# State space branch of a hybrid decoder kernel kept with features on partitions, its norm factors spread by rows through DRAM

## The chip, the cores and the metric

One core of one Trainium2 chip runs the whole program. The metric is device time in microseconds (us), the median of repeated runs. Beside it stands one execution that the hardware profiler took. TensorE is called PE here, VectorE DVE, ScalarE ACT, GpSimd POOL; SP is the engine whose queue issues nearly all DMAs. A weight load is PE's fetch of a matmul's stationary operand.

## What is computed

A decoder trunk of two layers on 512 tokens of width 1024, in float32. Each layer projects the normed input once, feeds three branches (a state space branch, latent attention, a gated delta rule), merges them by sigmoid gates, and ends with a feed-forward block. The change lies in the state space branch:

```python
def ssd_mixer(z, xbc, dt_raw, conv_w, conv_b, dt_bias, a_log, d_skip, norm_g):
    xbc = jax.nn.silu(causal_dwconv(xbc, conv_w) + conv_b)
    xs, bm, cm = jnp.split(xbc, [SSD_INNER, SSD_INNER + G * N], axis=-1)
    dt = jax.nn.softplus(dt_raw + dt_bias).reshape(Bsz, S, G, E)
    a = -jnp.exp(a_log).reshape(G, E)
    y = ssd_chunked(xs * dt[..., None], dt * a, bm, cm)
    y = y + d_skip.reshape(G, E)[:, :, None] * xs
    y = y.reshape(Bsz, S, SSD_INNER) * jax.nn.silu(z)
    y = rmsnorm(y.reshape(Bsz, S, G, SSD_INNER // G), norm_g.reshape(G, SSD_INNER // G))
```

There are G = 2 groups of E = 8 heads of width 64, state width 128, and four chunks of 128 tokens. In a chunk the output is the sum of a part inside it (decay matrix times the product of `cm` and `bm`, times `xs * dt`) and a part from the state carried in (`cm` times state, times the decay since the chunk's start). The norm runs over the 512 features of a group, so it needs one factor for each token and group.

## The kernel before, in words

**Dense products.** Weights come in pieces of 512 KB by a DMA on SP's queue (`weights_raw`, L161, two buffers `wraw`). `split_half` makes of each half piece a high and a low part, `whi` by a copy on ACT (L154) and `wlo` by a subtraction on DVE (L155), four buffers each. `mm3` then issues three matmuls of 512 columns for each pair of 128x128 blocks (L182, L183, L184); these rows are called dense here. `dense_F` puts output features on partitions (the weights are the stationary operand), `dense_T` puts tokens there.

**The state space branch** is `ssd_group(g)`, called for g = 0 and 1 in each of two layers, four calls in all. It first projects `bm` and `cm` and, tile by tile, `xs`, with features on partitions; a convolution and SiLU follow (`conv_silu`, L682 to L686, `silu2`, L262 and L263). Four transposes on PE (L720) and a copy on ACT (L721) turn each tile of `xs` so that tokens are on partitions. The gate `z` is projected with `dense_T` (`silu_T`) and has tokens on partitions too.

Then four chunks t follow. `seg_exp` fetches cumulated log decays from DRAM tensor `d_c`, spread over all partitions (L448), and makes the decay matrices `eE` on ACT (L450, L451). PE multiplies `bm` by `cm` (L733); DVE masks the product and multiplies it into `eE` (L735, L737). DVE makes `xd`, that is `xs` times step size (L739), and the skip term (L744). For each of eight heads PE multiplies with `eE` as stationary and 64 columns of `xd` as moving operand (L742), so the result has tokens on partitions; DVE adds it (L745). From the second chunk on, one matmul of 512 columns brings in the state (L748), which DVE scales by a column of decays and adds (L750, L751). `xe` (L754) and one matmul of 512 columns (L756) make the next state (L759, L761, L762). At a chunk's end DVE multiplies into `z` (L764), and ACT squares it and sums along the row in the same instruction (L766), which gives the norm's sum for each token.

After the chunks `rsq` makes the factors with one DVE instruction and a power on POOL (L258, L259). DVE scales `z` (L770). Then the result is turned back, four transposes a tile on PE (L775), and `split_gain` makes high and low parts in `yh` and `yl` (L254, L255).

**What sets the order.** A scheduler at build time places the instructions of all branches in each engine's queue; every engine then works strictly through its own queue. The buffers of `yh` and `yl` hold latent attention's outputs until its output projection has read them, so the turned results of the branch wait for the end of that projection, and group 0's results stay in the `tok` buffers meanwhile. Around the chunks stand dense rows of attention's output projection (`out_proj`) and, after it, of the gated delta rule's keys.

Of the kernel before, what the change touches and what calls it, by code (L numbers as in the profile page):

```python
# [20 lines left out]
P = 128  # L21
S = 512
# [12 lines left out]
ROWS = ('ssd_dt_bias', 'gdn_dt_bias', 'ssd_a_log', 'gdn_a_log', 'ssd_d')  # L35
# [20 lines left out]
def hybrid_kernel(ctx, tc, a, out, depth=2, taps=None):  # L56
# [42 lines left out]
    ct = mk(cst, [P, NBLK * P + 104], F32, "ct")  # L99
# [195 lines left out]
    def load_params(ly, rows=True):  # L295
        pc = mk(sp, [P, 155], F32, "pc", 2)
        sync.dma_start(pc, a["pcols"][ly])
        prow = mk(sp, [P, 64], F32, "prow", 2)
        if rows:
            load_rows(prow, ly)  # L300
        return pc, prow
# [49 lines left out]
    for ly in range(depth):  # L351
# [5 lines left out]
        sconv_b, g_n1, g_ssd, g_q, g_kv, g_gdn, g_n2 = 0, 12, 20, 28, 32, 34, 35  # L357
# [32 lines left out]
        d_c = mk(dr, [T, 24 * P], F32, "d_c", 2)  # L390

        def step_sizes():
# [35 lines left out]
            sync.dma_start(d_c.rearrange("t (n l) -> (t n) l", l=P), rows)  # L428
            dec = mk(sp, [P, 3, T, 24], F32, "dec")
# [8 lines left out]
            dsk = mk(sp, [P, 16], F32, "dsk")  # L438
            dve.tensor_scalar(dsk, prow[:, 48:64], 0.25, None, ALU.mult)
# [257 lines left out]
        def ssd_group(g, yh, yl):  # L697
            h0 = 8 * g
            xs = mk(br, [P, T, 512], F32, "tok", 4)
            z = mk(br, [P, T, 512], F32, "tok", 4)  # L700
# [13 lines left out]
            for cp in range(2):  # L714
                for j, pj in enumerate(dense_F(weights(w_in, O_XBC + 512 * g + 256 * cp, 256, D), tiles(256), D, xh, xl)):
                    xf = mk(br, [P, S], F32, "ft4", 2)
                    conv(pj, 4 * g + 2 * cp + j, xf)
                    ps = sm_bank()
                    for t in range(T):
                        pe.transpose(ps[:, t * P : (t + 1) * P], xf[:, t * P : (t + 1) * P], ident)  # L720
                    act.copy(xs[:, :, (2 * cp + j) * P : (2 * cp + j + 1) * P], ps.rearrange("p (t n) -> p t n", t=T))  # L721
            silu_T(br, O_SZ + 512 * g, z)

            hv8 = lambda x: x.rearrange("p (h n) -> p h n", h=8)
            ss = mk(sp, [P, T], F32, "sss")
            st = None
            for t in range(T):
# [10 lines left out]
                xd = mk(br, [P, 512], F32, "wk0")  # L738
                dve.tensor_tensor(hv8(xd), hv8(xs[:, t, :]), bc_last(dtq[:, t, h0 : h0 + 8], 64), ALU.mult)  # L739
                py = sm_bank()  # L740
                for h in range(8):
                    pe.matmul(py[:, h * 64 : (h + 1) * 64], e2[h // 4][:, h % 4, :], xd[:, h * 64 : (h + 1) * 64], start=True, stop=True)  # L742
                y = mk(br, [P, 512], F32, "wk1")
                dve.tensor_tensor(hv8(y), hv8(xs[:, t, :]), bc_last(dsk[:, h0 : h0 + 8], 64), ALU.mult)  # L744
# [559 lines left out]
```

## Time and profile before

| | us |
|---|---|
| median of 3 runs (lowest, highest) | 2334.94 (2334.29, 2338.41) |
| the profiled execution | 2335.61 |
| its span, first to last instruction | 2333.8 |
| PE busy | 2290.0 |
| DVE busy | 1585.9 |
| ACT busy | 1177.4 |
| POOL busy | 59.1 |

So 1.8 us of the profiled execution lie outside its span. Matmuls are pipelined: a record's duration is longer than the time until the next one may start. What a matmul costs in a full queue is read from the distance between two starts. A float32 matmul leaves two records, a dense one (rounded float32) and a transpose one. The form `64*64 64x64` names the part of the array that a matmul uses (rows*columns), then the shape.

### The profile page before, as it was taken

The page shows a single profiled execution, that of the slowest core. Times are in us where ns is not written, and L with a number is a line of the kernel's source. Part 1 is how long each engine was busy: PE and PEld are TensorE (multiplying, and loading weights), DVE is VectorE, ACT ScalarE, POOL GpSimd, SP SyncE. Part 2 cuts the span into 40 slices and gives each one's busy share as a digit, 9 for nine tenths or more (in the row PEclk, how much of TensorE's full clock was granted, in tenths as well). Part 3 has the DMA queues.
Part 4 walks back from the last instruction along what each step waited for, and adds up shares of the span by engine and source line. Part 5 has one row for each costly group of instructions (what it writes and reads, how often), then busy time and mean ns, then how long its engine had stood idle before and what let it go on. Part 6 is the DMA issues. An engine that isn't in the chain of part 4 may idle for free.

```text
span 2333.8 us, 32026 instructions
## 1 busy us (share of the span) xinstructions
PE 2290.0 (98%) x11814; PEld 1884.8 (81%) x11814; DVE 1585.9 (68%) x3116; ACT 1177.4 (50%) x2455; POOL 59.1 (3%) x74
## 2 busy tenths in 40 slices
PE   8999999999999999999999999999999999999998
PEld 7878788878887888888887787888788878888886
DVE  7776666775665458767867765667656645677668
ACT  6666644333443345554656667443334434545545
POOL 0000000000000000000000000000000000000000
PEclk9999999999999999999999999999999999999999
DMA  4223533442222443233132235334422224333231
GB/s 136 83 73 91 171 100 109 122 132 79 80 78 69 148 144 109 74 116 118 51 97 72 74 99 163 105 103 140 115 83 85 68 80 155 127 117 100 91 109 46
DMA packets 208702, 239.85 MB, mean 103 GB/s; under 512 B 33888, under 2 KB 157472, under 8 KB 208544
## 3 DMA queue, kind: packets, MB, share of 16 engines
q1 hardware_dynamic: 205344, 233.07, 33.0%
q10 hardware_dynamic: 3200, 4.72, 0.8%
q8 instruction: 93, 1.52, 0.3%
q14 instruction: 65, 0.53, 0.1%
HBM read 221.41 MB, written 11.63 MB: 100 GB/s over the span
## 4 chain that ended last, share of the span: by engine, by line
PE 88%; DVE 6%; DMA 2%; ACT 2%; POOL 1%; issue 1%; ACTq 0%; SPq 0%; DVEq 0%; POOLq 0%
PE acc L182 23%; PE acc L183 22%; PE acc L184 22%; PE sm L182 2%; PE sm L184 2%; PE sm L183 2%; DVE wlo L155 1%; PE sm L742 1%; DMA eE<-d_c 1%; PE sm L645 1%; DVE tok L858 1%; DVE gQ L857 1%; PE sm L1015 1%; POOL gms L259 1%; PE yt L661 1%
## 5 line engine op out<-in xcount | busy, mean ns | idle before, releaser
L155 DVE TENSOR_TENSOR wlo<-wraw,whi 128x512 fp32r<-128x512 f32 (+1 forms) x552 | 376.5, 686 | 421.7 <-ACT whi L154 407.1
L154 ACT CAST whi<-wraw 128x512 fp32r<-128x512 f32 (+1 forms) x552 | 339.9, 618 | 593.4 <-PE acc L183 384.2
L184 PE MATMUL acc<-xh,wlo 128*128 128x512 f32 (+1 forms) x1248 | 486.3, 390 | 0.0
L182 PE MATMUL acc<-xh,whi 128*128 128x512 f32 (+1 forms) x1248 | 486.0, 390 | 0.0
L183 PE MATMUL acc<-xl,whi 128*128 128x512 f32 (+1 forms) x1248 | 484.6, 389 | 1.0 <-issue 1.0
L184 PEld LDWEIGHTS acc<-xh,wlo 128*128 128x128 f32 x1248 | 235.6, 189 | 45.7 <-issue 1.2
L183 PEld LDWEIGHTS acc<-xl,whi 128*128 128x128 f32 x1248 | 235.7, 189 | 44.2 <-DVE xl L255 0.4
L182 PEld LDWEIGHTS acc<-xh,whi 128*128 128x128 f32 x1248 | 235.2, 189 | 43.7 <-ACT xh L254 0.4
L182 PE MATMUL acc<-yh,whi 128*128 128x512 f32 x384 | 151.9, 399 | 0.0
L183 PE MATMUL acc<-yl,whi 128*128 128x512 f32 x384 | 151.4, 394 | 0.0
L184 PE MATMUL acc<-yh,wlo 128*128 128x512 f32 x384 | 151.2, 394 | 0.0
L686 DVE SCALAR_TENSOR_TENSOR ckl<-acc,pc,ckl 128x511 f32<-128x511 f32 (+2 forms) x168 | 120.2, 743 | 15.5 <-ACT ckl L682 8.2
L154 ACT CAST whi<-wr 128x512 fp32r<-128x512 f32 x128 | 79.5, 621 | 66.6 <-PE acc L184 30.3
L184 PE MATMUL acc<-whi,xl 128*128 128x512 f32 (+1 forms) x288 | 111.3, 386 | 0.0
L183 PE MATMUL acc<-wlo,xh 128*128 128x512 f32 (+1 forms) x288 | 111.1, 386 | 0.0
L182 PE MATMUL acc<-whi,xh 128*128 128x512 f32 (+1 forms) x288 | 110.3, 385 | 0.0
L182 PE MATMUL acc<-whi,yh 128*128 128x512 f32 x256 | 99.7, 390 | 0.0
L184 PE MATMUL acc<-whi,yl 128*128 128x512 f32 x256 | 99.7, 389 | 0.0
L183 PE MATMUL acc<-wlo,yh 128*128 128x512 f32 x256 | 99.6, 389 | 0.0
L155 DVE TENSOR_TENSOR wlo<-wr,whi 128x512 fp32r<-128x512 f32 x128 | 86.0, 685 | 12.2 <-ACT whi L154 11.6
L182 PEld LDWEIGHTS acc<-yh,whi 128*128 128x128 f32 x384 | 71.7, 188 | 16.8 <-ACT yh L254 1.7
L183 PEld LDWEIGHTS acc<-yl,whi 128*128 128x128 f32 x384 | 72.2, 188 | 15.2 <-issue 1.0
(418 smaller groups left out, 4520.9 us busy)
## 6 DMA issues: line engine op xcount, KB each, us to landing
wraw<-in_w_in_dram SPq DMA_DIRECT2D x144, 512.0 KB, 3.6
wraw<-in_w_up_dram SPq DMA_DIRECT2D x64, 512.0 KB, 3.6
wr<-in_w_down_dram SPq DMA_DIRECT2D x32, 1024.0 KB, 5.0
eE<-d_c SPq DMA_DIRECT2D x48, 256.0 KB, 4.0
wraw<-in_w_mla_out_dram SPq DMA_DIRECT2D x16, 512.0 KB, 3.4
eE<-d_e SPq DMA_DIRECT2D x32, 256.0 KB, 3.1
wraw<-in_w_ssd_out_dram SPq DMA_DIRECT2D x16, 512.0 KB, 3.4
wraw<-in_w_gdn_out_dram SPq DMA_DIRECT2D x16, 512.0 KB, 3.4
```

The lines of the kernel that those rows point to most:

```text
L154: act.copy(hi, raw)
L155: dve.tensor_tensor(lo, raw, f32(hi), ALU.subtract)
L182: pe.matmul(o, ah, bh, start=start, stop=False, skip_group_check=more)
L183: pe.matmul(o, ah, bl, start=False, stop=False, skip_group_check=more)
L184: pe.matmul(o, al, bh, start=False, stop=stop, skip_group_check=more)
L259: pool.tensor_tensor(o, o, (exp if exp is not None else nhalf)[:, : o.shape[1]], ALU.pow)
L645: pe.transpose(ps[:, n : n + P], pn[t][:, kb * P : (kb + 1) * P], ident)
L661: pe.matmul(o, v_h, th[:, c : c + w], start=kb == 0, stop=False)
L686: dve.scalar_tensor_tensor(acc[:, d:], ps[:, : S - d], taps_[3 - d], acc[:, d:], ALU.mult, ALU.add)
L742: pe.matmul(py[:, h * 64 : (h + 1) * 64], e2[h // 4][:, h % 4, :], xd[:, h * 64 : (h + 1) * 64], start=True, stop=True)
L857: dve.tensor_tensor(pd, bc_last(nb[:, m, m + 1 :], m + 1), bc_mid(xb[:, m, : m + 1], 31 - m), ALU.mult)
L858: dve.tensor_tensor(xb[:, m + 1 :, : m + 1], xb[:, m + 1 :, : m + 1], pd, ALU.add)
```

## The change

`ssd_group` keeps its results with features on partitions from end to end.

- The transposed tile of `xs` is multiplied by the step size straight out of PSUM on DVE (L725, in place of the copy on ACT) and kept as `xd`; the untransposed tile is scaled by the skip factor on ACT (L727). The skip factors come as a column for each feature (`dsk`, L443).
- `z` is projected with `dense_F`, 256 features at a time.
- For each head PE now has 64 columns of `xd` as stationary and 128 columns of `eE` as moving operand (L751). Heads in even places go to partitions 0 to 63 of the result, odd ones to 64 to 127: matmuls of form 128*64, in two positions.
- The state's part is four matmuls of 128 columns (L760). Its decays now differ along the row, so they are written to DRAM once a layer (`d_p`, L431, L432) and fetched with two DMAs of 64 partitions for each of chunks 1 to 3 (L757, buffers `wk0` and `wk1`); DVE multiplies (L761).
- The norm's sum is over partitions now: ACT squares (L778), DVE folds four tiles into one (L779, L780), and a matmul with a column of ones sums it (L781). The factors, one for each partition, are transposed (L785), copied (L787), written to DRAM (`d_r`, L788) and fetched by one DMA spread over all partitions (L790).
- The 16 transposes at a call's end go, and so does the scaling of L770. Instead DVE multiplies each tile by gain and factors into the buffer of `yl` of the next number (L794), from where `split_act` makes `yh` and `yl` (L250, L251). The buffers `yh` and `yl` are taken one by one there and no longer all at once.
- There are five `tok` buffers in place of four.

```diff
             for cp in range(2):
                 for j, pj in enumerate(dense_F(weights(w_in, O_XBC + 512 * g + 256 * cp, 256, D), tiles(256), D, xh, xl)):
...
-                    act.copy(xs[:, :, (2 * cp + j) * P : (2 * cp + j + 1) * P], ps.rearrange("p (t n) -> p t n", t=T))
-            silu_T(br, O_SZ + 512 * g, z)
+                    th = lambda x: x.rearrange("p t (h n) -> p t h n", h=2)
+                    dve.tensor_tensor(th(xd[:, :, c * P : (c + 1) * P]), th(ps.rearrange("p (t n) -> p t n", t=T)),
+                                      bc_last(dtq[:, :, h0 + 2 * c : h0 + 2 * c + 2], 64), ALU.mult)
+                    act.activation(xf[:, c, :], xf[:, c, :], AF.Copy, scale=dsk[:, 4 * g + c : 4 * g + c + 1])
+            for cp in range(2):
+                for j, pj in enumerate(dense_F(weights(w_in, O_SZ + 512 * g + 256 * cp, 256, D), tiles(256), D, xh, xl)):
+                    silu2(z[:, 2 * cp + j, :], pj)
...
-                xd = mk(br, [P, 512], F32, "wk0")
-                dve.tensor_tensor(hv8(xd), hv8(xs[:, t, :]), bc_last(dtq[:, t, h0 : h0 + 8], 64), ALU.mult)
                 py = sm_bank()
-                for h in range(8):
-                    pe.matmul(py[:, h * 64 : (h + 1) * 64], e2[h // 4][:, h % 4, :], xd[:, h * 64 : (h + 1) * 64], start=True, stop=True)
-                y = mk(br, [P, 512], F32, "wk1")
-                dve.tensor_tensor(hv8(y), hv8(xs[:, t, :]), bc_last(dsk[:, h0 : h0 + 8], 64), ALU.mult)
-                dve.tensor_tensor(y, y, py, ALU.add)
+                for c in range(4):
+                    for i in range(2):
+                        h = 2 * c + i
+                        pe.matmul(py[64 * i : 64 * i + 64, c * P : (c + 1) * P], xd[:, t, h * 64 : (h + 1) * 64], e2[h // 4][:, h % 4, :], start=True, stop=True)
+                y = xf[:, :, tok]
+                dve.tensor_tensor(y, y, c4(py), ALU.add)
                 if t > 0:
+                    eb = mk(br, [P, 4, P], F32, f"wk{t % 2}")
+                    for i in range(2):
+                        sync.dma_start(eb[64 * i : 64 * i + 64], d_p.rearrange("t (n l) -> t n l", l=P)[t, h0 + i : h0 + 8 : 2].partition_broadcast(64))
                     po = sm_bank()
-                    pe.matmul(po, ctl[:, tok], st, start=True, stop=True)
...
+                    for c in range(4):
+                        pe.matmul(po[:, c * P : (c + 1) * P], st[:, c * P : (c + 1) * P], ctl[:, tok], start=True, stop=True)
+                    dve.tensor_tensor(eb, c4(po), eb, ALU.mult)
+                    dve.tensor_tensor(y, y, eb, ALU.add)
...
-                dve.tensor_tensor(z[:, t, :], z[:, t, :], y, ALU.mult)
-                jk = mk(br, [P, 512], F32, "wk2")
-                act.activation(jk, z[:, t, :], AF.Square, accum_out=ss[:, t : t + 1])
+                zt = z[:, :, tok]
+                dve.tensor_tensor(zt, zt, y, ALU.mult)
+                sq = mk(br, [P, 4, P], F32, "wk2")
+                act.activation(sq, zt, AF.Square)
+                dve.tensor_tensor(sq[:, 0:2], sq[:, 0:2], sq[:, 2:4], ALU.add)
+                dve.tensor_tensor(sq[:, 0], sq[:, 0], sq[:, 1], ALU.add)
+                pe.matmul(pss[:, t : t + 1], sq[:, 0], ones[:, 0:1], start=True, stop=True)
             rs = mk(sp, [P, T], F32, "srs")
-            rsq(rs, ss, 1.0 / 512, EPS)
-            for t in range(T):
-                dve.tensor_scalar(z[:, t, :], z[:, t, :], rs[:, t : t + 1], None, ALU.mult)
+            rsq(rs, pss[:, :T], 1.0 / 512, EPS)
+            ps = sm_bank()
+            pe.transpose(ps[:T, :P], rs, ident)
+            rsT = mk(br, [T, P], F32, "gk", 2)
+            act.copy(rsT, ps[:T, :P])
+            sync.dma_start(d_r[g].rearrange("(t p) -> t p", p=P), rsT)
+            rb = mk(br, [P, S], F32, "ft4", 2)
+            sync.dma_start(rb, d_r[g].partition_broadcast(P))
             for c in range(4):
                 k = 4 * g + c
-                ps = y_bank()
-                for t in range(T):
-                    pe.transpose(ps[:, t * P : (t + 1) * P], z[:, t, c * P : (c + 1) * P], ident)
-                split_gain(yh[k], yl[k], ps, col(g_ssd + k))
+                yn = mk(lp, [P, S], F32, f"yl{k + 1}") if k < KD - 1 else z[:, c, :]
+                dve.scalar_tensor_tensor(yn, z[:, c, :], col(g_ssd + k), rb, ALU.mult, ALU.mult)
+                yh.append(mk(lp, [P, S], F32R, f"yh{k}"))
+                yl.append(mk(lp, [P, S], F32R, f"yl{k}"))
+                split_act(yh[k], yl[k], yn)
```

The scheduler orders the queues anew. On PE's queue, at the second chunk of group 0 in the first layer, there stands before (`eE` is the decay matrix, `ckh` holds `bm` and `cm`, `st` the state, `kt` the transposed `bm`):

```order
L184 MATMUL acc_2983<-xh_30_146,wlo_3022 128x512
L742 MATMUL sm_2766<-wk_656_2764,eE_2744 128x64 x4
L742 MATMUL sm_2766<-wk_656_2764,eE_2745 128x64 x4
L748 MATMUL sm_2778<-st_2739,ckh_563_2264 128x512
L756 MATMUL sm_2785<-wk_661_2783,kt_2265 128x512
L733 MATMUL sm_2807<-ckh_563_2264,ckh_562_2263 128x128
L182 MATMUL acc_2983<-xh_31_147,whi_3021 128x512
```

and of the change, at the same place (`tok` is `xd`, `wk_633` the folded squares of the chunk before):

```order
L184 MATMUL acc_2984<-xh_28_144,wlo_3004 128x512
L751 MATMUL sm_2753<-eE_2733,tok_2251 64x128
L781 MATMUL yt_2690<-ct_75,wk_633_2728 128x1
L751 MATMUL sm_2753<-eE_2733,tok_2251 64x128 x3
L760 MATMUL sm_2766<-ckh_551_2254,st_2725 128x128 x2
L751 MATMUL sm_2753<-eE_2734,tok_2251 64x128 x4
L760 MATMUL sm_2766<-ckh_551_2254,st_2725 128x128 x2
L767 MATMUL sm_2775<-wk_641_2773,kt_2255 128x512
L742 MATMUL sm_2800<-ckh_551_2254,ckh_550_2253 128x128
L182 MATMUL acc_2984<-xh_29_145,whi_3003 128x512
```

The eight matmuls of the heads no longer stand together: the sum of squares of the chunk before and the state's part cut them into three pieces. Over the four chunks of a call they lie in 1, 3, 2 and 3 pieces.

Also on PE's queue, behind the last chunk of that group, there stands before (`tok` is the scaled result, `yt` its transpose):

```order
L184 MATMUL acc_3058<-yh_541_2236,wlo_3112 128x512
L775 MATMUL yt_2891<-ct_75,tok_2262 128x128
L182 MATMUL acc_3131<-xh_26_142,whi_3135 128x512
L775 MATMUL yt_2891<-ct_75,tok_2262 128x128
L183 MATMUL acc_3131<-xl_34_150,whi_3135 128x512
```

and of the change (`yt` now holds the sums, `srs` the factors; 20 dense rows, the first row here the last of them, stand between the chunk's last L760 and this L781):

```order
L184 MATMUL acc_3057<-yh_450_1864,wlo_3096 128x512
L781 MATMUL yt_2690<-ct_75,wk_663_2880 128x1
L182 MATMUL acc_3058<-yh_424_1764,whi_3095 128x512
L183 MATMUL acc_3058<-yl_425_1765,whi_3095 128x512
L184 MATMUL acc_3058<-yh_424_1764,wlo_3096 128x512
L785 MATMUL sm_2888<-ct_75,srs_2885 4x128
L182 MATMUL acc_3058<-yh_450_1864,whi_3095 128x512
```

The first transposes of the result are gone from here; the last sum and, three dense rows behind it, the transpose of the factors have come in. The change's rows are alike in all four calls, here and above; the interleaved transposes of before stand only behind group 0 of each layer, since group 1's come later.

On SP's queue, between the weights of the output projection, the change puts there (`gk` is the factors' transposed copy, `ft` their spread form; the rows of `d_e` and `d_c` belong to the gated delta rule's decays):

```order
L161 DMA wraw_3207<-in_w_mla_out_dram 128x4x256
L788 DMA d_r_448<-gk_2890 4x128
L821 DMA d_e_2249<-eE_2935 128x512
L821 DMA d_e_2249<-eE_2943 128x512
L790 DMA ft_667_2893<-d_r_448 128x512
L452 DMA eE_2967<-d_c_446 128x512
L821 DMA d_e_2249<-eE_2951 128x512
L452 DMA eE_2975<-d_c_446 128x512
L161 DMA wraw_3241<-in_w_mla_out_dram 128x4x256
```

Everything behind L790, the next piece of weights among it, is issued only after the write of L788 has landed.

52 lines of the change are left out of this document (27 added, 25 removed).

## The prediction

> **What bounds the kernel.** I read the page first, for who is busy and what the chain of waits is made of.
>
> ```profile
> span 2333.8 us, 32026 instructions
> PE 2290.0 (98%) x11814; PEld 1884.8 (81%) x11814; DVE 1585.9 (68%) x3116; ACT 1177.4 (50%) x2455; POOL 59.1 (3%) x74
> PE 88%; DVE 6%; DMA 2%; ACT 2%; POOL 1%; issue 1%; ACTq 0%; SPq 0%; DVEq 0%; POOLq 0%
> ```
>
> PE is busy for 98% and makes up 88% of the chain, so a microsecond of PE work taken out or put in is a microsecond of the result, unless it falls into a wait. Next I read the stretch that the change rewrites, the four chunks of the first call, by busy time of PE, weight loads, DVE, ACT and POOL, granted clock and DMA.
>
> ```profile
> 236.00:270.00 34.00, 33.39 (x170) 25.93 (x168) 27.15 (x46) 22.50 (x59) 0.66 (x1) 1.00 0.50 151
> ```
>
> And PE's waits in it (total, times, longest):
>
> ```profile
> PE yt L775 <- DVE tok L770: 0.7, 1, 0.7
> PE sm L742 <- DVE eE L737: 0.6, 1, 0.6
> ```
>
> PE is idle for 0.6 of 34 us at full clock, while DVE works 27. It waits 0.6 us for the masked decay matrix and, at the stretch's end, 0.7 for the scaled result. So DVE has little to give back here, and the sum is one of PE's queue. I price each kind of matmul by distances between starts.
>
> **Transposes of the result (L775): out.** The timeline shows one tile's four among dense rows.
>
> ```profile
> 412.23 0.39 PE L182 MATMUL acc<-xh,whi 128*128 128x512 f32 x1
> 412.46 0.60 PE L775 MATMUL yt<-ct,tok 128*128 128x128 f32 x4
> 412.81 0.48 PE L183 MATMUL acc<-xl,whi 128*128 128x512 f32 x1
> 413.13 0.39 PE L184 MATMUL acc<-xh,wlo 128*128 128x512 f32 x1
> ```
>
> The group's row has count, busy time, mean ns and PE's wait ahead of it:
>
> ```profile
> L775 PE MATMUL yt<-ct,tok 128*128 128x128 f32 x64 | 10.9, 277 | 1.3 <-DVE tok L770 1.3
> ```
>
> From 412.23 to 413.13 pass 0.90 us; two dense steps at 0.23 (412.23 to 412.46) are 0.46, so four transposes cost 0.44. Sixteen tiles make **-7.0**. The 1.3 us in the group's row, PE's wait for L770, go too: **-1.3**.
>
> **The heads' matmuls (L742 becomes L751).** Before, eight heads leave 16 records.
>
> ```profile
> 243.09 1.90 PE L742 MATMUL sm<-wk,eE 128*128 128x64 f32 x16
> 244.83 1.08 PE L748 MATMUL sm<-st,ckh 128*128 128x512 f32 x2
> 245.74 1.02 PE L756 MATMUL sm<-wk,kt 128*128 128x512 f32 x2
> 617.39 1.05 PE L1015 MATMUL sm<-wk,eE 128*128 128x128 f32 x8
> 618.28 1.03 PE L1020 MATMUL sm<-st,ft 128*128 128x256 f32 x4
> ```
>
> The 16 take 1.74 us (243.09 to 244.83), 0.109 a record, 27.8 us over 16 chunks. A record of 128 columns takes 0.89/8 = 0.111 (617.39 to 618.28), so one behind another the new ones would gain nothing: twice the columns, half the stationary operand. But they lie in two halves of the array. No row shows this form; the nearest are three matmuls on three of 16 parts, of which two (one L907 and the L908) read partitions 32 to 63 and so stand on the same array rows, differing in columns alone, as the new pair does.
>
> ```profile
> 1677.47 0.22 PE L907 MATMUL sm<-wk,ft 32*32 32x32 f32 x2
> 1677.49 0.21 PE L908 MATMUL sm<-ft,wk 32*32 32x32 f32 x1
> 1677.53 0.20 PE L907 MATMUL sm<-wk,ft 32*32 32x32 f32 x2
> 1677.54 0.19 PE L908 MATMUL sm<-ft,wk 32*32 32x32 f32 x1
> 1677.56 0.20 PE L907 MATMUL sm<-wk,ft 32*32 32x32 f32 x2
> 509.39 1.20 PE L891 MATMUL sm<-wk,tok 32*32 32x32 f32 x64 [1.88 <-DMA wk<-d_x]
> ```
>
> All three start within 0.02 us, and the next three come 0.03 later (1677.53 to 1677.56). Records pass in step, one on each part. So I let a pair cost one record. With pieces of 8; 1, 3 and 4; 4 and 4; 4, 1 and 3 heads a call needs 8, 10, 8 and 10 such slots (an odd head has none beside it): 36 slots of 0.111, 4.0 us; four calls 16.0. That is **-11.8**; with no pairing it is 256 records, 28.4, or +0.6. These are the ends; I take the first, as the rows at 1677 are nearest in what matters, the shared rows.
>
> The Trainium skill speaks against this end: "TensorE: Matmul & The Clock Gate", Part 3, under "The mechanism", says that a weight load overlaps matmuls in flight only if it targets another group of rows; both halves here use all rows. The rows at 1677 disagree, since two parts on the same rows keep the pace of 0.03 us with their loads. The same part gives 2.38x for three column parts; as an estimate from it, two would run 1.6x as fast, and the term would be -10 or so.
>
> **Changing the form.** Whenever PE leaves 128*128 and comes back, something is lost.
>
> ```profile
> 541.52 0.39 PE L184 MATMUL acc<-yh,wlo 128*128 128x512 f32 x1
> 541.84 1.14 PE L929 MATMUL sm<-tok,kt 64*64 64x64 f32 x16
> 542.91 0.50 PE L182 MATMUL acc<-xh,whi 128*128 128x512 f32 x1
> 543.25 0.39 PE L183 MATMUL acc<-xl,whi 128*128 128x512 f32 x1
> ```
>
> From 541.52 to 543.25 pass 1.73 us; less 0.46 for dense steps, 1.27 remain for 16 records. If a record streams half of 0.111, as half the columns should, 0.89 to 0.94 is work, so the visit costs 0.34. The order shows 36 pieces in form 128*64: **+12.2**. Bounds: nothing (their neighbours are often float32 matmuls, not dense ones), and 0.45 each if a weight load of 0.11 is laid bare besides, +16.2. I take 0.34, the only measured row. So the heads' pairing pays for its visits and no more: **+0.4 together**.
>
> **State part (L748 becomes L760).** Two records of 512 columns took 0.91 (244.83 to 245.74); eight of 128 take 0.89. Twelve times: **-0.2**. `z`, projected the other way, keeps its 96 matmuls a call and its weights: 0.
>
> **Sums and factors (L781, L785).** The same kind of sum, wait and power stands in latent attention's query.
>
> ```profile
> 64.89 0.39 PE L182 MATMUL acc<-ckh,whi 128*128 128x512 f32 x1
> 65.12 0.95 PE L531 MATMUL sm<-ct,pn 128*128 128x1 f32 x8
> 65.93 0.49 PE L182 MATMUL acc<-cqh,whi 128*128 128x512 f32 x1
> 66.25 0.40 PE L183 MATMUL acc<-ckl,whi 128*128 128x512 f32 x1
> 66.10 0.16 DVE L258 TENSOR_SCALAR qrs<-sm 128x4 f32<-128x4 f32 x1 [1.62 <-PE sm L531]
> 66.35 1.01 POOL L259 TENSOR_TENSOR qrs<-qrs,nhalf 128x4 f32<-128x4 f32 x1 [12.63 <-DVE qrs L258]
> ```
>
> 1.36 less 0.46 is 0.90 for eight records, 0.113 each; L781 has two: 16 x 0.225 = **+3.6**. L785 is a transpose (0.11) in form 128*32, so one visit more: 4 x 0.45 = **+1.8**. And PE waits there. The last record of L531 starts about 65.9, the power ends at 67.36: the factors come 1.5 us after the sum. PE has three dense rows between, 0.9 with the step into them. **+2.4** for four waits of 0.6; bounds 0 (the wait hides the change of form) and 6.
>
> **Waits for the sum (L781).** PE reaches the last sum of a call 20 dense rows after the state part, 4.6 us. The way there is longer than before:
>
> ```profile
> L744 DVE TENSOR_TENSOR wk<-tok,dsk 128x512 f32<-128x512 f32 x3 | 2.1, 684 | 0.0
> ```
>
> That is the group's row in the chunks' stretch; these are from the timeline:
>
> ```profile
> 268.34 0.63 ACT L766 ACTIVATE wk<-tok 128x512 f32<-128x512 f32 x1
> 270.38 1.68 DVE L770 TENSOR_SCALAR tok<-tok,srs 128x512 f32<-128x512 f32 x4 [0.53 <-POOL srs L259]
> ```
>
> Four DVE instructions of this size and one `wlo` among them, 3.4; the square, 0.63; two folds of half and a quarter of that size, 0.5: some 4.8 us with the signals between. So I put 0.2 on each of four, **+0.8**, and nothing on the other twelve; the bounds are 0 and 0.7 on each of 16 (one more DVE instruction ahead), +11. Waiting behind a waiting L781 are dense rows, that is, everything.
>
> **DVE, ACT and DMA.** In a chunk DVE loses L739 and L744 (1.37) and gains the folds (0.5); four scalings of 0.42 go at the end (L770, 270.38). L725 comes instead where `xs` is made, and L794 and L251 replace one L255 a tile later. PE gets back at most its waits of the second table, 0.6 to 1.3 a call; I take **-1.0** in all, bounds 0 and -5. ACT swaps a copy for a scaling (L727) and casts for activations: 0, covered by dense rows.
>
> ```profile
> eE<-d_c SPq DMA_DIRECT2D x48, 256.0 KB, 4.0
> d_c<-crow SPq DMA_DIRECT2D x2, 48.0 KB, 1.9
> ```
>
> The 24 fetches of L757 are issued a chunk or more ahead. Factors need a write (about 1.9) and a spread read (4.0): with copy and issue some 9 us after the sum. In group 1 DVE's first L794 waits for them, and `wlo` stands behind it. By then four half pieces of weights (four buffers), 12 dense rows or 2.7 us each, are split ahead, enough for 11 us from the end of the projection before; the sum lies 19 dense rows, 4.4 us, ahead of that end. So the wait is covered by some 6 us, and costs its excess once that cover is gone. On SP the write's 1.9 us holds back L161, again behind 11 us of split weights: 0.
>
> **Sum.** -7.0 - 1.3 + 0.4 - 0.2 + 3.6 + 1.8 + 2.4 + 0.8 - 1.0 = -0.5 us, against 2335.61 of the profiled execution. That is 0.67 above the median of 2334.94, so I forecast **2334.5**.
>
> **Rivals.**
>
> *Changes of form are cheap.* If a visit costs 0.1 (its neighbours load float32 weights anyway, and L781 hides in it), 40 visits give back 9.6: 2325. For it: L531's eight records show no loss at all when kinds change inside one form. Against it: L929. Chance 0.20, faster.
>
> *PE waits at the sums: slower.* A sum now sits on PE's own strict queue, where before ACT summed as a by-product. One DVE instruction of 0.69 more ahead of the folds, at each of 16 sums, is +10 beyond the forecast: 2344. It decides as soon as the way to L781 is longer than the rows ahead of it, and these are within 0.2 us of each other at a call's end. For it: DVE is busy 27 of 34 us. Against it: the 1.4 us a chunk that DVE loses. Chance 0.25, slower.
>
> *Halves do not pair* (the skill's rule, by its mechanism here: each record waits for the one in the other half). Then the heads cost +0.6 in place of -11.8: 2347. Against it: the rows at 1677. Chance 0.10, slower. In none of the cases does the change fail to do what it says: the order has the 64 transposes out.
>
> **Numbers.** The forecast's case has 0.45, with 2329 to 2341 for its own range. Within 0.2% (4.7 us, about what a measurement of this kernel can tell from no change) it leaves 0.35; 0.06 of it is faster, 0.04 slower. With the rivals: faster 0.26, same 0.35, slower 0.39. The range for 8 in 10 reaches to both sides' cases, 2325 to 2347.
>
> **What would show it.** Right: L751's starts in twos within 0.02 us, about 0.9 for eight heads that stand together; PE idle ahead of L785 by 0.6; 128*64 pieces costing 0.3 above their records. Wrong: L751 evenly 0.11 apart; idle ahead of L781 for DVE L780 or ACT L778 in every chunk; PE waiting for `wlo` behind L794.

## The result, and the profile after

| | before | after |
|---|---|---|
| median in us (runs) | 2335.35 (6) | 2328.63 (6) |
| lowest and highest | 2333.94, 2338.41 | 2326.75, 2331.10 |
| ratio, 95% interval | | 0.9976 (0.9966 to 0.9986) |
| the profiled execution | 2335.61 | 2326.75 |

The change makes the kernel faster by 0.24%, 6.7 us. The forecast was 2334.5 in a range of 2325 to 2347; its likeliest case ended at 2329. Two later comparisons of the same two kernels gave 0.9956 (0.9943 to 0.9969) and 0.9977 (0.9968 to 0.9985). They differ because an execution catches none, one or several stretches of half granted clock, most worth 1.7 or 5 us each; the last section shows them. In the second of the two the runs of both kernels had the same mean granted clock (0.9975 changed, 0.9974 before); in the first it was 0.9983 against 0.9962, a difference worth up to 5 us of the span.

The page of the changed kernel, span and busy time:

```profile
span 2325.0 us, 32170 instructions
PE 2282.8 (98%) x11858; PEld 1876.3 (81%) x11858; DVE 1589.2 (68%) x3132; ACT 1175.7 (51%) x2445; POOL 58.9 (3%) x74
```

PE has 7.2 us less to do, and is still the bound. Next the first call's chunks, by busy time of PE, weight loads, DVE, ACT and POOL, clock and DMA; the window runs, like that of before, from ahead of the first chunk to behind the last.

```profile
235.90:269.40 33.50, 32.96 (x193) 24.48 (x192) 25.18 (x48) 20.79 (x52) 1.01 (x1) 1.00 0.57 169
```

Before, 34.00 us had 33.39 of PE and 27.15 of DVE; that window holds 87 dense rows, this one 83, so part of DVE's difference is the shorter window. Over the whole span DVE has 3.3 us more to do than before (1589.2 against 1585.9). PE's waits from 200 to 1620 us, which take in all four calls (total, times, longest), of before:

```profile
PE sm L742 <- DVE eE L737: 2.6, 4, 1.3
PE sm L891 <- DMA wk<-d_x: 1.9, 1, 1.9
PE yt L775 <- DVE tok L770: 1.3, 2, 0.7
```

and of after:

```profile
PE sm L785 <- POOL srs L259: 2.3, 4, 0.6
PE sm L912 <- DMA wk<-d_x: 1.7, 1, 1.7
```

The two waits of the branch are gone, 3.9 us in all, and one new one is there, for the factors, 2.3. No wait for a masked decay matrix is left, and none for a folded square (L780), as far as this view goes: it lists waits from 0.15 us on.

The first chunk on PE, with the heads in one piece:

```profile
236.86 0.39 PE L183 MATMUL acc<-xl,whi 128*128 128x512 f32 x1
237.18 1.09 PE L751 MATMUL sm<-eE,tok 128*64 128x128 f32 x16
238.21 1.13 PE L767 MATMUL sm<-wk,kt 128*128 128x512 f32 x2
239.17 0.38 PE L742 MATMUL sm<-ckh,ckh 128*128 128x128 f32 x2
239.62 0.39 PE L182 MATMUL acc<-xh,whi 128*128 128x512 f32 x1
```

The trace's single records behind the second row start in twos, 0.007 us apart, and a new pair every 0.109 us (237.450 and 237.457, 237.559 and 237.566). From 237.18 to 238.21 the eight heads take 1.03; before, 16 records took 1.74. Last, the end of a call: the square, its folds, the sum, the power and the transpose.

```profile
264.37 0.63 ACT L778 ACTIVATE wk<-tok 128x512 f32<-128x512 f32 x1 [2.09 <-DVE tok L776]
265.03 0.42 DVE L779 TENSOR_TENSOR wk<-wk 128x256 f32<-128x256 f32 x1 [0.69 <-ACT wk L778]
265.49 0.29 DVE L780 TENSOR_TENSOR wk<-wk 128x128 f32<-128x128 f32 x1
265.56 0.39 PE L184 MATMUL acc<-yh,wlo 128*128 128x512 f32 x1
265.93 0.35 PE L781 MATMUL yt<-ct,wk 128*128 128x1 f32 x2
266.32 0.16 DVE L258 TENSOR_SCALAR srs<-yt 128x4 f32<-128x4 f32 x1
266.56 1.01 POOL L259 TENSOR_TENSOR srs<-srs,nhalf 128x4 f32<-128x4 f32 x1 [199.99 <-DVE srs L258]
266.68 0.40 PE L184 MATMUL acc<-yh,wlo 128*128 128x512 f32 x1
267.62 0.27 PE L785 MATMUL sm<-ct,srs 128*4 128x128 f32 x1 [0.54 <-POOL srs L259]
```

The sum starts 0.37 behind the dense row ahead of it, 0.14 later than a step of 0.23. The transpose starts 0.94 behind its dense row: 0.71 of that is the wait for POOL.

### The profile page after: what moved, and what is told of

It reads as the page before. It is cut to its first block, busy times and chain, and to the rows that moved or that the text cites. A ratio compares the mean times of both kernels' runs of the same rounds, so it can differ in the third digit from the quotient of the medians.

```text
span 2325.0 us, 32170 instructions
## 1 busy us (share of the span) xinstructions
PE 2282.8 (98%) x11858; PEld 1876.3 (81%) x11858; DVE 1589.2 (68%) x3132; ACT 1175.7 (51%) x2445; POOL 58.9 (3%) x74
## 4 chain that ended last, share of the span: by engine, by line
PE 87%; DVE 6%; ACT 2%; DMA 2%; POOL 1%; issue 1%; ACTq 0%; SPq 0%; DVEq 0%; POOLq 0%
PE acc L182 22%; PE acc L183 22%; PE acc L184 22%; PE sm L183 2%; PE sm L182 2%; PE sm L184 2%; DVE wlo L155 1%; PE sm L751 1%; DVE tok L879 1%; PE sm L649 1%; DVE gQ L878 1%; PE sm L1036 1%; POOL gms L259 1%; ACT whi L154 1%; PE sm L760 1%
## 5 line engine op out<-in xcount | busy, mean ns | idle before, releaser
L184 PE MATMUL acc<-xh,wlo 128*128 128x512 f32 (+1 forms) x1376 | 535.3, 389 | 0.0
L182 PE MATMUL acc<-xh,whi 128*128 128x512 f32 (+1 forms) x1376 | 534.2, 389 | 0.0
L183 PE MATMUL acc<-xl,whi 128*128 128x512 f32 (+1 forms) x1376 | 533.5, 388 | 0.2 <-DVE xl L255 0.2
L183 PEld LDWEIGHTS acc<-xl,whi 128*128 128x128 f32 x1376 | 258.9, 188 | 49.4 <-DVE xl L255 0.8
L184 PEld LDWEIGHTS acc<-xh,wlo 128*128 128x128 f32 x1376 | 258.9, 188 | 49.1
L182 PEld LDWEIGHTS acc<-xh,whi 128*128 128x128 f32 x1376 | 258.5, 188 | 48.9 <-ACT xh L254 0.4
L184 PEld LDWEIGHTS acc<-yh,wlo 128*128 128x128 f32 x384 | 72.2, 188 | 14.5
L454 ACT ACTIVATE eE<-eE,cum 128x128 f32<-128x128 f32 x192 | 63.1, 390 | 22.4 <-DMA eE<-d_c 19.3
L1236 DVE TENSOR_TENSOR h<-h,acc 128x512 f32<-128x512 f32 x96 | 61.6, 681 | 0.0
```

What stands on the lines that cost most here:

```text
L182: pe.matmul(o, ah, bh, start=start, stop=False, skip_group_check=more)
L183: pe.matmul(o, ah, bl, start=False, stop=False, skip_group_check=more)
L184: pe.matmul(o, al, bh, start=False, stop=stop, skip_group_check=more)
L454: act.activation(o[:, i], o[:, i], AF.Relu, scale=-1.0, bias=cum[:, t, h0 + i : h0 + i + 1])
L1236: dve.tensor_tensor(hs_, hs_, ps[t], op)
```

## The experiments

The theory after the result: (a) two halves of the array pass in step and pay for the heads; (b) a visit to form 128*64 costs about 0.28 us; (c) DVE's smaller load took PE's waits away; (d) the sums on PE's queue wait only at a call's end. Ratios are to the kernel before, from runs on the same chip; a difference of two ratios is turned into us with 2333. The line numbers in a run's rows are those of its own kernel.

The medians carry the chance of the half clock. The traces give a second measure: the time between the same dense rows on both sides of the two layers' branch stretches (from the 600th to the 1700th and from the 5000th to the 5900th of 8736), both stretches together. No half clock falls into them but in experiments 3 and 8, where it costs up to 6.8 us. Three traces of the changed kernel agree within 0.2 us.

| kernel | us between the dense rows |
|---|---|
| before | 539.1 |
| changed, three traces | 531.9, 532.0, 532.1 |
| experiments 1, 2, 3, 4 | 539.5, 529.8, 549.1, 532.5 |
| experiments 6, 7, 8 | 537.9, 528.5, 547.0 |
| experiments 10, 11, 12 | 532.2, 525.4, 525.1 |

**1. Heads not in twos** (e1_unpaired).

```diff
-                for c in range(4):
-                    for i in range(2):
+                for i in range(2):
+                    for c in range(4):
                         h = 2 * c + i
```

> Emits the heads of even places first, then the odd ones, so that neighbours on PE's queue stand in the same half of the array; the number of pieces (36) stays. If two halves pass in step (the pairing theory), eight heads need about 15 slots of 0.11 us in place of 8: about 24 slots more a call, +10.5 us against the changed kernel (2328.6), so about 2339, and the piece of eight at a call's first chunk takes about 1.7 us from its first start to the next instruction's instead of 1.0. If the gain came from shorter streaming or a smaller stationary operand and not from pairs, nothing changes: 2328.6.

Measured: ratio 0.9992 (0.9984 to 1.0001), +3.7 us against the changed kernel's 0.9976. The piece of eight in the first chunk:

```profile
236.11 1.58 PE L751 MATMUL sm<-eE,tok 128*64 128x128 f32 x16
237.62 1.12 PE L767 MATMUL sm<-wk,kt 128*128 128x512 f32 x2
```

1.51 us in place of 1.03. The records show four alone, then four pairs, then four alone: 12 slots of 0.109, where 16 were to be expected without any pairing, 15 by my count, and 8 with it. The pairs in the middle fit odd heads that start while the last four records of the even ones are not done; the records do not name their half, so this is an inference. Over the four calls the chunks' time on PE (below: blocks) grows by 6.3 us, and with a new wait of 0.8 for a sum and 0.5 more at the factors' transposes it is 7.6 between the dense rows; 10.5 was expected. So (a) holds; the full price of no pairing was not reached by this edit.

**2. Heads kept together** (e2_whole).

```diff
-                for c in range(4):
-                    for i in range(2):
-                        h = 2 * c + i
-                        pe.matmul(py[64 * i : 64 * i + 64, c * P : (c + 1) * P], xd[:, t, h * 64 : (h + 1) * 64], e2[h // 4][:, h % 4, :], start=True, stop=True)
+                with tc.high_priority():
+                    for c in (2, 3, 0, 1):
+                        for i in range(2):
+                            h = 2 * c + i
+                            pe.matmul(py[64 * i : 64 * i + 64, c * P : (c + 1) * P], xd[:, t, h * 64 : (h + 1) * 64], e2[h // 4][:, h % 4, :], start=True, stop=True)
```

> Keeps the eight heads of a chunk together (16 pieces in place of 36; nothing is left out). If a visit to form 128*64 costs 0.29 us, 20 visits fewer are -5.8 and the pairs that single heads lost -1.7: about 2321. At the forecast's 0.34 it is -8.5 (2320), at the cheap rival's 0.1 it is -3.7 (2325). Another theory: PE now waits for the second decay matrix before the whole piece, at 0.3 to 0.7 in each chunk from the second on, which eats it: 2325 to 2329.

Measured: 2321.31 us, ratio 0.9955 (0.9943 to 0.9968); the changed kernel had 0.9956 to 0.9977 in its three comparisons, so by the medians the gain is 0 to 5 us and not clear; between the dense rows it is 2.1. The last chunk of the first call, in the changed kernel:

```profile
257.88 0.39 PE L182 MATMUL acc<-yh,whi 128*128 128x512 f32 x1
258.19 0.66 PE L751 MATMUL sm<-eE,tok 128*64 128x128 f32 x8
258.78 0.71 PE L760 MATMUL sm<-ckh,st 128*128 128x128 f32 x4
259.42 0.43 PE L751 MATMUL sm<-eE,tok 128*64 128x128 f32 x2
259.79 0.38 PE L781 MATMUL yt<-ct,wk 128*128 128x1 f32 x2
260.10 0.65 PE L751 MATMUL sm<-eE,tok 128*64 128x128 f32 x6
260.68 0.71 PE L760 MATMUL sm<-ckh,st 128*128 128x128 f32 x4
261.46 0.39 PE L184 MATMUL acc<-yh,wlo 128*128 128x512 f32 x1
```

and here:

```profile
257.12 0.39 PE L184 MATMUL acc<-yh,wlo 128*128 128x512 f32 x1
257.44 1.09 PE L752 MATMUL sm<-eE,tok 128*64 128x128 f32 x16
258.46 0.49 PE L761 MATMUL sm<-ckh,st 128*128 128x128 f32 x2
258.82 0.35 PE L782 MATMUL yt<-ct,wk 128*128 128x1 f32 x2
259.03 0.91 PE L761 MATMUL sm<-ckh,st 128*128 128x128 f32 x6
260.02 0.39 PE L183 MATMUL acc<-yl,whi 128*128 128x512 f32 x1
```

From the dense row ahead to the second one behind: 3.58 there, 2.90 here. That is 0.68 for two visits and two slots less (0.22), 0.23 a visit; the quickest of the four such blocks has 0.11 less, 0.28 a visit. Visits are priced, and (b) holds. Where the gain of 20 visits went stand these waits of the same stretch, 200 to 1620 us:

```profile
PE sm L786 <- POOL srs L259: 3.2, 4, 0.8
PE sm L752 <- DVE eE L746: 2.8, 4, 0.8
PE yt L782 <- DVE wk L781: 1.6, 2, 0.9
```

7.6 us against 2.5 in the changed kernel (2.3 for L785 and 0.2 for L751): 5.1 of some 7 were given back in waits, 4.2 of them behind DVE, by the second theory's mechanism. The 2.8 for the masked matrix speak against (c): DVE's smaller load is all there, and with the heads in one piece, second half first, the wait is as long as the 2.6 of before.

**3. Factors written without a transpose** (e3_colwrite).

```diff
-            ps = sm_bank()
-            pe.transpose(ps[:T, :P], rs, ident)
-            rsT = mk(br, [T, P], F32, "gk", 2)
-            act.copy(rsT, ps[:T, :P])
-            sync.dma_start(d_r[g].rearrange("(t p) -> t p", p=P), rsT)
+            sync.dma_start(d_r[g].rearrange("(t p) -> p t", p=P), rs)
```

> The norm's factors are written to DRAM straight from their columns, four bytes at a time; their transpose on PE (L785) and its copy are gone. If the transpose with its wait for POOL costs PE 0.85 us each, four of them give -3.4 against the changed kernel: about 2325. Rival: the small pieces make the write slow (over 6 us instead of 2), SP's queue and DVE's first multiply by factors come late, and PE waits for weights: 2329 or more.

Measured: 2337.49 us, ratio 1.0027 (1.0016 to 1.0039), 12 us slower than the changed kernel. The rival is right. The DMA issue (KB, us to landing):

```profile
d_r<-srs SPq DMA_DIRECT2D x4, 2.0 KB, 9.1
```

and, from 260 to 420 us, what SP's queue waited for:

```profile
SPq L786 <- DMA d_r<-srs: 16.4, 2, 8.6
```

2 KB in 4-byte pieces take 9.1 us; SP waits for them twice in this window, and PE then for `whi`, 7.6 us over both layers, 3.9 at the longest.

**4. One more DVE instruction ahead of each sum** (e4_dve).

```diff
                 dve.tensor_tensor(zt, zt, y, ALU.mult)
+                dve.tensor_tensor(zt, zt, zt, ALU.max)
```

> One more DVE instruction of 128x512 (an idle maximum of the gated tile with itself) in each chunk ahead of the square. The rival of the prediction, sums on PE's strict queue with no slack: +0.69 at each of 16 sums, +10 or more: 2339. The theory after the result: only the last sum of a call has no slack (it already shows 0.13 to 0.20 of idle), so four waits of about 0.7: +2.8, about 2331.5, and no idle ahead of the other twelve.

Measured: 2326.22 us, ratio 0.9976 (0.9966 to 0.9987), no different from the changed kernel. The sums' waits, 200 to 1620 us:

```profile
PE yt L782 <- DVE wk L781: 1.3, 2, 1.0
```

Wait for a sum shows twice, 1.3 us in all (one of 1.0 and one of 0.2 in the two layers), not 16 times. The rival of +10 falls, and even my +2.8 is too much: 0.4 to 0.6 between the dense rows. The planner knows the added instruction and puts the sums of the inner chunks later. (d) holds for this order only.

**5. The changed kernel again** (e5_again, no edit).

> The changed kernel itself once more, as the line that the other kernels are measured against, and for its trace around 510 us, where the kernel before lost about 4 us to a granted clock of 0.5 to 0.6 behind a wait of PE for a DMA (L891) and the changed kernel did not, at the same place. If that clock belongs to the kernel before, it stays at 1.00 here; if it is chance, it can be low here too. Time: 0.9966 to 0.9986 of the kernel before.

Measured: 2322.11 us, ratio 0.9956 (0.9943 to 0.9969), below what was expected. Its profiled execution kept clock 1.00 around 510 us, and had no half clock anywhere before the end. The kernels of experiments 1, 3, 10 and 11, which are the changed one but for small edits, had it there. So the low clock does not belong to the kernel before.

**6. The kernel before with less for DVE** (e6_b_light).

```diff
-                xd = mk(br, [P, 512], F32, "wk0")
-                dve.tensor_tensor(hv8(xd), hv8(xs[:, t, :]), bc_last(dtq[:, t, h0 : h0 + 8], 64), ALU.mult)
+                xd = xs[:, t, :]
...
-                dve.tensor_tensor(hv8(y), hv8(xs[:, t, :]), bc_last(dsk[:, h0 : h0 + 8], 64), ALU.mult)
-                dve.tensor_tensor(y, y, py, ALU.add)
+                dve.tensor_tensor(y, xs[:, t, :], py, ALU.add)
```

> The kernel before, with step size and skip factor left out of the chunks (xd is xs itself, y is xs plus the heads' result): DVE is spared L739 and L744, 1.37 us a chunk. If PE's waits for the masked decay matrix (L742 behind L737, together 3.6 us) came from DVE's load, they go: -3 to -4 us against the kernel before, ratio about 0.9985. If they came from ACT or the fetches of the decays, nothing changes: 1.000.

Measured: ratio 0.9977 (0.9968 to 0.9986), -5.4 us (-3.3 to -7.5). Its waits for `eE` behind the masking, 2.6 us in the view of before (the expectation's 3.6 is not in it), are gone. From 200 to 1620 us another wait has grown, the one ahead of the transposes, from 1.3:

```profile
PE yt L773 <- DVE tok L768: 2.8, 2, 1.6
```

So the -5.4 is not the price of two DVE instructions. Between the dense rows this kernel saves 1.3 us: what the heads no longer wait is in good part waited ahead of the transposes. The rest lies outside the branch: its runs had a mean granted clock of 0.9985 against 0.9962 of the kernel before beside them, worth up to 5 us of the span, and one wait for a DMA (L889, L891 before) was 0.8 in place of 1.9. (c) holds for the waits at the heads, at about 1 us net, and not for 3. This kernel's chunks also moved 5 to 18 dense rows ahead in PE's queue, which the planner ordered anew; the two effects were not parted.

**7. The kernel before without the transposes of its result** (e7_b_noturn).

```diff
-                ps = y_bank()
-                for t in range(T):
-                    pe.transpose(ps[:, t * P : (t + 1) * P], z[:, t, c * P : (c + 1) * P], ident)
-                split_gain(yh[k], yl[k], ps, col(g_ssd + k))
+                split_gain(yh[k].rearrange("p (t n) -> p t n", t=T), yl[k].rearrange("p (t n) -> p t n", t=T), z[:, :, c * P : (c + 1) * P], col(g_ssd + k))
```

> The kernel before, with the 64 transposes of the result (L775) left out: the high and low parts are made from the unturned tile, so features and tokens are mixed up. If they cost what their rows say, 7.0 us and 1.6 of waiting for L770, this is -8.6: ratio 0.9963. If PE only waits elsewhere in their place (for the weights' parts, or the next branch), -2 to -4: 0.9985 or so.

Measured: ratio 0.9962 (0.9949 to 0.9975), -8.9 us, and -10.6 between the dense rows. The rows' price holds, and nothing takes the transposes' place. 1.5 of the 10.6 are waits for the masked matrix, which fall from 2.6 to 1.1 (0.6 and 0.5 in the two layers) though every DVE instruction of the chunks is still there; so these waits hang on the order too. The other 9.1 are the transposes with their wait.

**8. Heads together, and the small pieces on POOL's queue** (e8_whole_pool; besides the edit of experiment 2).

```diff
-            sync.dma_start(d_r[g].rearrange("(t p) -> t p", p=P), rsT)
+            pool.dma_start(d_r[g].rearrange("(t p) -> p t", p=P), rs)
...
-            sync.dma_start(rb, d_r[g].partition_broadcast(P))
+            pool.dma_start(rb, d_r[g].partition_broadcast(P))
```

> Eight heads together as in the second experiment, and the factors written from their columns as in the third, but write and fetch are issued on POOL's queue, so that SP's weights do not stand behind them; nothing is left out. If the third's loss came from SP's queue alone, the transpose with its wait (about 1.05 us each there) goes for nothing: -4.2 against the second experiment, ratio to the kernel before about 0.9937. If DVE's first multiply by the late factors holds up the weights' low parts, PE waits for them and it is no faster than the second: 0.9955 or more.

Measured: 2340.24 us, ratio 1.0031 (1.0020 to 1.0042): as slow as the third. POOL's queue does not help. In the window from 272 to 276 us (PE, weight loads, DVE, ACT, POOL, clock, DMA share, GB/s):

```profile
272.00:276.00 4.00, 4.00 (x19) 3.30 (x18) 0.69 (x1) 1.21 (x3) 0.00 (x0) 1.00 0.34 26
```

and of the changed kernel at that time:

```profile
272.00:276.00 4.00, 4.00 (x20) 3.30 (x19) 1.37 (x3) 3.11 (x9) 0.00 (x0) 1.00 0.78 246
```

While the pieces are written, 26 GB/s move in place of 246, and SP waits long for the landing of a transfer that has nothing to do with them (8.3 us at the longest; in the changed kernel 3.2): SP from 262 to 292 us, DVE and PE from 395 to 420 us of the eighth kernel.

```profile
SPq L452 <- DMA d_e<-eE: 13.6, 6, 8.3
```

```profile
DVE tok L791 <- DMA ft<-d_r: 11.1, 1, 11.1
```

```profile
PE acc L184 <- DVE wlo L155: 2.5, 1, 2.5
```

The last two are group 1's: DVE's first multiply waits 11.1 us for the factors, and PE 2.5 for the weights' low part behind it. That is the chain whose cover the prediction put at some 6 us beyond 9; with the write at 9.5 us in place of the forecast's 1.9 it breaks, as it should.

**9 and 10. The changed kernel, and its transpose three dense rows later** (e9_again, no edit; e10_late: what follows the sums from the transpose on becomes a function, called inside the output projection).

```diff
...
-        out_proj(a["w_mla_out"][ly], 1, *y_mla, br, (0, 1))
+        out_proj(a["w_mla_out"][ly], 1, *y_mla, br, (0, 1), after=at(7, tail))
...
```

> The changed kernel a third time, as the base for the three kernels beside it on the same chip. Expected: 0.9956 to 0.9976 of the kernel before, with a median of 2322 to 2328 that depends on how many stretches of half granted clock its runs catch.

> The transpose of the factors (L785) stands six dense rows behind the last sum in place of three; else PE's queue is the same, and nothing is left out. If its cost is mostly PE's wait for POOL (0.7 of 0.85 us), the wait goes: -2.8 us against the changed kernel on the same chip, and its own cost falls to 0.2 to 0.4 each. If the wait hides the change of form, as the lower bound of the prediction has it, only -1.5; if the factors' later arrival makes DVE's first multiply hold up the weights, 0 or slower.

Measured: 0.9977 (0.9968 to 0.9985) and 0.9980 (0.9970 to 0.9991): no gain that can be told, nor between the dense rows (532.2 against 532.1); -2.8 was expected. On PE the four transposes fell from 3.4 to 0.68 us together, as expected of the wait. What ate it was, in the first layer, from 270 to 345 us,

```profile
PE sm L715 <- DVE ft L263: 2.4, 1, 2.4
```

and ahead of it SP's L789, the write of the factors, which stood 4.1 us for the late copy with the next weights behind it; ACT then waited 3.3 us for a piece of weights. That this chain is the cause is read from these waits and was not tested. The profiled execution also had 12.0 us of its span lost to half clock, against 1.7 of the kernel beside it.

**11 and 12. Late transpose, fewer pieces, masks first** (e11_late_whole adds experiment 2's edit to what follows; e12_late_fwd leaves the heads in their order).

```diff
-                for e in e2:
-                    dve.tensor_tensor(e, e, bc_mid(cb, 4), ALU.mult)
+                with tc.high_priority():
+                    for e in e2:
+                        dve.tensor_tensor(e, e, bc_mid(cb, 4), ALU.mult)
```

> The late transpose, the eight heads of a chunk together (16 pieces), and DVE's products of mask and decays taken ahead of its other work; nothing is left out. The second experiment gained 7 us of PE time by fewer pieces but showed waits of 0.7 to 0.95 for the second decay matrix in most later chunks and about 1.0 ahead of the transposes. If these waits go with the order of DVE and the later transpose, -6 to -9 against the changed kernel: ratio to the kernel before about 0.993. If the wait only moves on to the sums or to the weights' low parts, -1 to -3.

> The late transpose and DVE's products of mask and decays first, with heads left in their order (20 pieces by the planner's own choice); nothing is left out. 16 visits fewer at 0.28 are -4.5, the transposes -2.8: -7 against the changed kernel if no wait comes in their place; -2 to -3 if PE waits for the second decay matrix inside the piece as in the second experiment.

Measured: 2323.55 us, 0.9958 (0.9946 to 0.9970), and 2321.05 us, 0.9944 (0.9930 to 0.9958), beside 2326.08 us and 0.9977 of the changed kernel on the same chip. The twelfth is faster than both kernels: its interval lies below the changed kernel's of 0.9968 to 0.9985, by 5 us in the medians and 6.9 between the dense rows, as expected. The eleventh gains 2.5 in the medians, which does not part it from the changed kernel, and 6.6 between the dense rows. The profiled executions lost 5.1 (twelfth) and 6.8 us (eleventh) to half clock ahead of the last dense rows, that of the changed kernel beside them 1.7. With DVE's products ahead of its other work PE's waits for them are 1.3 us in the four calls, in place of 2.8 in experiment 2's kernel; in the eleventh, with experiment 2's 16 pieces, they are 1.7. The twelfth has a wait of 1.3 at its sums instead (L782 behind ACT's L454). The eleventh has 1.8 us of the tenth's wait at L715. Its transposes and the twelfth's wait for nothing; the twelfth's first shows what a bare one costs:

```profile
267.66 0.39 PE L184 MATMUL acc<-yh,wlo 128*128 128x512 f32 x1
267.89 0.27 PE L787 MATMUL sm<-ct,srs 128*4 128x128 f32 x1
267.91 0.48 PE L182 MATMUL acc<-yh,whi 128*128 128x512 f32 x1
268.23 0.40 PE L183 MATMUL acc<-yl,whi 128*128 128x512 f32 x1
```

0.57 from 267.66 to 268.23, less 0.46: 0.11, a record and no change of form.

## Why the prediction was right, and which sizes were off

The result lies in the range, 5.9 us below the forecast and 0.4 below its likeliest case. That it lies inside owes something to the width of the range, 22 us: the forecast's sum of -0.5 said that no change would be told, and "faster" had 0.26, the least of the three chances. The costs on PE's queue came as they were described, and the three signs of being right showed (starts in twos, idle ahead of L785, 0.28 a visit); the sum fell short in the sizes of four terms, and for one of them, DVE, the mechanism stays open. Blocks are measured from the dense row ahead of them to the second one behind, less two steps of 0.228 us, and summed over the four calls of the profiled executions.

| term | forecast | measured |
|---|---|---|
| transposes L775 and their wait | -8.3 | -9.2 |
| chunks with heads, visits, state, sums, waits | +3.6 | -0.5 |
| transpose of the factors and its wait | +4.2 | +3.4 |
| transposes of `xs` (L720, L723) | 0 | -0.3 |
| sum | -0.5 | -6.6 |

Between the dense rows named above the change saves 3.2 and 4.0 us in the two layers; 0.6 of these 7.2 are in no block and stay unassigned.

- **Transposes out, -7.0 and -1.3**: right, 0.9 too small. Most of that are the eight transposes of group 0 that stand one by one between dense rows, as the order of before shows: each costs 0.20 there, not 0.11. Experiment 7 finds about the same, 9.1.
- **Pairs, -11.8**: right. L751 starts in twos and takes 0.109 a pair. The Trainium skill's rule ("TensorE: Matmul & The Clock Gate", Part 3, "The mechanism"), by which a weight load overlaps only across groups of rows, does not hold here: both halves use all 128 rows, each pair has its own two loads, and the pace is that of one record.
- **Changing the form, +12.2**: mis-sized by 2. The first chunk's block is 239.62 less 236.86 less 0.46, 2.30; less 0.89, 0.91 and 0.22 for its records that leaves 0.28 for a visit, not 0.34, and experiment 2 agrees. 36 of them are 10.1. The rival "changes of form are cheap" reached nearly the right time by the wrong cause: 0.1 a visit is not what the rows show.
- **DVE, -1.0**: mis-sized. It took PE's waits from one chunk stretch, 0.6, and allowed them to go at 0.6 to 1.3 a call, but booked 1.0 in all. The waits behind L737 were 2.6 in the four calls, and all went. Reading the wait over every call, and not the first only, would have shown the size. That DVE's smaller load took them is not shown: experiment 2 has that load and waits 2.8, experiment 7 has the old load and waits 1.1, and in experiment 6 they go with the load but the order changes too and the net gain is 1.3. Load, pieces and order each play in; what each is worth stays open.
- **L785, +1.8 and +2.4**: the wait was 0.7 and not 0.6; the visit to another form cost nothing. Its record shows 128*4, and experiment 12 shows it at 0.11 with no visit to pay: 1.4 too much, 0.6 too little.
- **Waits for sums, +0.8**: right, 0.13 to 0.20 at each call's end. The rival of +10 fell in experiment 4.
- **DMA and the cover of 6 us**: right as far as shown. PE never waits for `wlo` behind L794 in the changed kernel, and experiment 8, whose write takes 7.6 us more than forecast, breaks the cover; its size was not measured.

Of the 4 us that the chunks came out lower, 2.1 are visits and 1.6 the waits behind L737; 0.4 stay spread.

## What to carry to other kernels

Two matmuls with 64 columns of stationary operand run for the price of one (0.109 us a pair here) if they go to both halves of the array and stand near each other in the queue, but every return to the full array costs (0.28 us here); so keep such matmuls in one piece, and look first at what the piece will wait for. When an engine off the chain holds up the one on it, sum these waits over all repetitions before calling them small, and look after the change where they went: in experiments 2, 6 and 10 time taken from PE came back, in part or whole, as a wait at another place. A transfer of a few KB in 4-byte pieces is not small: 2 KB took 9.1 us on SP's queue and 9.5 on POOL's, which did not hide it. Where chance in the clock is as large as the effect, compare the time between the same rows of two traces beside the medians: by the medians experiment 6 is worth 5.4 us, by the rows 1.3.

## What the runs showed beside this

**Half clock after a wait.** The spread of the runs (2326.85 to 2337.24 for the kernel before on one chip) comes in the main from stretches in which PE's granted clock is half: over these 29 runs the span falls as the run's mean granted clock rises, from 0.994 to 0.999 (correlation -0.89). The profiled execution of before, from ahead of L891's wait on:

```profile
507.00:511.00 4.00, 2.12 (x69) 1.62 (x68) 0.08 (x1) 1.60 (x3) 0.00 (x0) 1.00 1.06 168
511.00:521.00 10.00, 10.00 (x176) 7.61 (x175) 4.45 (x8) 6.17 (x11) 0.00 (x0) 0.50 0.59 146
```

and of the changed kernel, behind another wait and at the same work:

```profile
143.80:147.20 3.40, 3.40 (x15) 2.90 (x16) 1.84 (x6) 2.05 (x7) 0.00 (x0) 0.51 0.39 136
508.00:518.00 10.00, 10.00 (x282) 7.89 (x282) 5.83 (x10) 6.97 (x13) 0.00 (x0) 1.00 0.68 154
```

After a wait of 1.9 us the clock halves for 10 us; after one of 1.7 it does not, and 4.3 us of the profiled executions' difference lie there. In the profiles of both kernels and of all twelve experiments such stretches, where there are any ahead of the last dense rows, last 3.4, 6.8 or 10.2 us, and each comes with or right behind PE idle of 1.1 to 3.9 us. The same waits come with and without it: around 510 us idle of 1.46 us had it (experiment 1) and of 1.72 not (the changed kernel). Leaving out half of each stretch, the profiled spans are 2328.7 before, 2321.6, 2319.3 and 2320.9 for the three of the changed kernel, and 2314.6 for the twelfth. The Trainium skill ("TensorE: Matmul & The Clock Gate", Part 1, "What's actually happening") tells of an activity window of 3413 ns that runs freely; the lengths of 3.4 us and its multiples agree, and a free window would explain why the same wait counts in one run and not in the next. That it takes a whole idle window does not agree with waits of 1.5 us. What decides it stays open.

**Parts in step.** If the reading of experiment 1 is right, records for the other half of the array start while four records ahead of them in the queue are not done: the ninth record of that piece in the queue's order starts 0.006 us behind the fifth. Between the two halves, then, PE does not work strictly through its queue, as was assumed ahead of the prediction.
